# Output product by halves, with seven products in place of eight

## The chip, the cores and the metric

The kernel runs on one core of one Trainium2 chip. The metric is the device time of one execution in microseconds. The engines named below are TensorE (PE, with PEld for its weight loads), VectorE (DVE), ScalarE (ACT), GpSimd (POOL) and SyncE (SP), which issues nearly all transfers.

## The reference

One layer of a decoder on a sequence of 4096 tokens of width 1024. A normalised and modulated input h is projected; three groups of heads mix it (sliding-window attention, RWKV-7 and gated linear attention), each is multiplied by its own SiLU gate, and the groups side by side go through one output projection:

```python
    y = jnp.concatenate([attn, rwkv, gla], axis=-1) @ w_out
    return x + gate[:, None] * _rmsnorm(y, g_post)
```

The change is about this product, [4096 x 1024] by [1024 x 1024].

## The kernel before

All work is tiled by 256 tokens, 16 tiles (NS). A first pass over the tiles computes h and the two recurrent mixers and writes h (hscr) and the mixers' output (mscr) to device memory; besides, its stage_c (line 856) prepares weights for the second pass, one block a tile: a block of 1024 x 256 is read in eight pieces, its squares are summed, it is scaled by a power of two and split into a high and a low f16 part, and both are written to wscr. Blocks 7 to 10 of these eleven are w_out.

The second pass computes, tile by tile, the projections for attention and gates from hT (qkv, line 1531; gates, line 1577), the attention (stage_s, line 1592), the gated mixture (stage_m, line 1666) and the output product with its norm (outp, line 1701). stage_p2 (line 1733) gives TensorE's order in one tile: outp of the tile before, gates of this tile, qkv of the next; the attention of stage_s and the small sum of stage_m are put between.

Every large matmul is three f16 matmuls into one PSUM tile: high by high, high by low, low by high. In outp the stationary operand is a 128 x 128 block of the gated mixture (mT, tokens by depth), the moving one 256 columns of w_out: for each of two token halves and four column blocks, eight slices of depth with three matmuls each (proj_tok, line 512). Two column blocks share a PSUM tile of 512 columns; there are two such tiles, tag pj, which gates and qkv use as well. ScalarE or VectorE scales each block by its own factor oi into yv; a square with a sum, a reciprocal root by steps (rsqrt, line 415), a multiplication by gn and the addition of x follow, and the row block is stored.

stage_m, ahead of it, loads mscr into the upper half of mx, multiplies by the gates (ag), sums the squares of the whole tile, forms a power of two from the sum (pow2, line 425) and splits mx into mT, two halves of depth at a time. All four blocks of w_out, high and low, stay in SBUF: eight loads at line 1760. gn, the product of the post norm's weight and the adaLN gate, is formed in stage_v (line 1504) from three loads issued by ScalarE.

The order on each engine is written out by hand: emit (line 533) runs the stages' generators against a model of the clock, every operation is noted with a rank (its place in the program plus a lag), and Order.pin goes through all operations with estimated durations, takes on each engine the one of lowest rank that is ready, and fixes that order by dependencies. It covers TensorE, VectorE, ScalarE, POOL and SP; a transfer that is issued by ScalarE directly (nc.scalar.dma_start) is not noted. Each engine, SP too, then works its list in order and waits where an operand is not there. A flag decides after the first pass whether a slow path for one mixer runs (tc.If); in these runs it doesn't.

## Time and profile before

| what | us |
|---|---|
| median of 3 runs | 2195.03 |
| lowest and highest run | 2191.54, 2196.71 |
| the profiled execution's own time | 2192.24 |
| its span, first to last instruction | 2190.5 |

The page gives busy times of one profiled execution of this program; its time is 1.7 us longer than its span and 2.8 us below the median. Times in views are microseconds from the span's start, durations of one instruction in nanoseconds. A matmul's duration holds its way through the array, so throughput is read from the distance of starts. Nearly all instructions bear line 319, the helper that records them: groups are told apart by the names of their tiles.

### The profile page before, as it was taken

The page shows a single profiled execution, that of the slowest core. Times are in us where ns is not written, and L with a number is a line of the kernel's source. Part 1 is how long each engine was busy: PE and PEld are TensorE (multiplying, and loading weights), DVE is VectorE, ACT ScalarE, POOL GpSimd, SP SyncE. Part 2 cuts the span into 40 slices and gives each one's busy share as a digit, 9 for nine tenths or more (in the row PEclk, how much of TensorE's full clock was granted, in tenths as well). Part 3 has the DMA queues.
Part 4 walks back from the last instruction along what each step waited for, and adds up shares of the span by engine and source line. Part 5 has one row for each costly group of instructions (what it writes and reads, how often), then busy time and mean ns, then how long its engine had stood idle before and what let it go on. Part 6 is the DMA issues. An engine that isn't in the chain of part 4 may idle for free. (4 is left out here: it accounts for less than half of the span.)

```text
span 2190.5 us, 61819 instructions
## 1 busy us (share of the span) xinstructions
PE 2075.6 (95%) x25469; PEld 1770.8 (81%) x25469; DVE 1486.5 (68%) x4959; ACT 1109.3 (51%) x2645; POOL 203.0 (9%) x404
## 2 busy tenths in 40 slices
PE   4999999999999999999887999999999999999996
PEld 4778877888887878877566888888888888888885
DVE  6677777777687776876645767656666666666764
ACT  3966676667675766665133434434343444433442
POOL 0011111111101111123500000000000000000000
PEclk9999999999999999999788999999999999999998
DMA  9232323132223231333333121111221211212111
GB/s 314 87 104 80 99 92 103 38 96 86 88 83 99 90 99 32 106 122 112 97 121 120 59 81 61 63 66 65 76 73 64 79 52 61 81 69 81 61 42 40
DMA packets 162420, 188.50 MB, mean 86 GB/s; under 512 B 49857, under 2 KB 133331, under 8 KB 157909
## 3 DMA queue, kind: packets, MB, share of 16 engines
q1 hardware_dynamic: 160100, 182.23, 25.3%
q8 instruction: 202, 3.31, 0.6%
q10 hardware_dynamic: 2032, 2.26, 0.3%
q14 instruction: 86, 0.70, 0.1%
HBM read 126.75 MB, written 57.68 MB: 84 GB/s over the span
## 5 line engine op out<-in xcount | busy, mean ns | idle before, releaser
L319 PEld LDWEIGHTS <-mT 128*128 128x128 f16 x3072 | 301.3, 98 | 39.1 <-ACT mT L319 2.6
L319 ACT ACTIVATE pr<-pr,nm,lsc 128x256 f32<-128x256 f32 (+1 forms) x256 | 149.3, 585 | 86.2 <-DVE nm L319 86.2
L319 ACT ACTIVATE ag<-gp,gh 128x512 f32<-128x512 f32 x64 | 43.6, 682 | 183.3 <-PE gp L319 183.3
L319 DVE CUSTOM_DVE_ANT_0 pr<-sc,ab,sinks 128x256 f32<-128x256 f32 (+1 forms) x256 | 107.7, 476 | 36.6 <-PE sc L319 34.6
L319 PEld LDWEIGHTS <-hT 128*128 128x128 f16 x1536 | 116.4, 98 | 18.6 <-DVE hT L319 1.7
L319 DVE SCALAR_TENSOR_TENSOR ag<-ag,gp 128x512 f32<-128x512 f32 x64 | 43.4, 678 | 111.6 <-ACT ag L319 111.5
L319 PE MATMUL pv<-gvh,hT 128*128 128x272 f16 x512 | 98.9, 282 | 0.9 <-DVE hT L319 0.8
L319 PE MATMUL qp<-hT,q1h 128*128 128x256 f16 x512 | 88.4, 278 | 8.3 <-DVE kT L319 8.3
L319 PE MATMUL op<-o0h,mT 128*128 128x256 f16 x512 | 93.3, 276 | 2.8 <-ACT mT L319 2.5
L319 POOL COPY kT<-kT 128x512 f16<-128x512 f16 x15 | 9.2, 612 | 923.8 <-DVE kT L319 859.4
L319 PE MATMUL zz<-hT,kh 128*128 128x256 f16 x512 | 93.1, 275 | 0.0
L319 ACT ACTIVATE jy<-yv 128x1024 f16<-128x1024 f32 x32 | 33.8, 1056 | 113.8 <-DVE yv L319 113.8
L319 PE MATMUL op<-o3h,mT 128*128 128x256 f16 x512 | 91.4, 273 | 0.0
L319 PE MATMUL gqk<-hT,gqkh 128*128 128x256 f16 x512 | 87.8, 273 | 3.4 <-DVE zb L319 2.7
L319 PE MATMUL op<-o2h,mT 128*128 128x256 f16 x512 | 89.3, 273 | 0.0
L319 PE MATMUL lp<-hT,Lh 128*128 128x256 f16 x512 | 89.0, 273 | 0.1
L319 PE MATMUL op<-o1h,mT 128*128 128x256 f16 x512 | 89.1, 273 | 0.0
L319 PE MATMUL zz<-hT,rh 128*128 128x256 f16 x512 | 89.1, 276 | 0.0
L319 PE MATMUL zz<-hT,vh 128*128 128x256 f16 x512 | 88.1, 273 | 0.0
L319 PE MATMUL gp<-hT,q3h 128*128 128x256 f16 x512 | 86.7, 275 | 0.0
L319 PE MATMUL qp<-hT,q0h 128*128 128x256 f16 x512 | 86.6, 275 | 0.0
L319 ACT ACT_TABLE_LOAD x65 | 83.4, 1283 | 5.3 <-DMA sinks<-in_rows 4.2
(416 smaller groups left out, 6365.4 us busy)
## 6 DMA issues: line engine op xcount, KB each, us to landing
xt<-in_x SPq DMA_DIRECT2D x16, 1024.0 KB, 5.7
hscr<-hT SPq DMA_DIRECT2D x16, 1024.0 KB, 5.1
hT<-hscr SPq DMA_DIRECT2D x16, 1024.0 KB, 4.8
xo<-in_x SPq DMA_DIRECT2D x16, 1024.0 KB, 5.6
out<-yv SPq DMA_DIRECT2D x32, 512.0 KB, 3.1
cs<-in_w SPq DMA_DIRECT2D x112, 128.0 KB, 2.2
cs<-in_wo SPq DMA_DIRECT2D x64, 128.0 KB, 2.3
v<-vscr SPq DMA_DIRECT2D x128, 64.0 KB, 1.9
```

The source lines that it names most:

```text
L319: r = f(*args, **kw)
```

## The change

Mixture and w_out are cut into halves, a11 to a22 (tokens by depth) and w11 to w22 (depth by columns), each product of a block pair is 128 tokens by 512 depth by 512 columns, and the eight block products become seven, of sums and differences (the Winograd form of Strassen's identity). Seven weight sets (w11, w21, w22, and four combinations) are formed in the first pass: wo_squares sums the squares of all of w_out in tiles 7 and 8, and wo_group forms, splits and writes a strip of 128 rows and 128 columns of each quarter, 16 groups in tiles 9 to 14, with four subtractions on POOL. One scale holds for all of w_out.

In the second pass stage_m keeps the mixture in two tiles (mxa, mxb), squares each half by itself, and forms four combinations of the token blocks on POOL, three of them in place. block splits one operand [128 x 4 x 128] into high and low; four such tiles go round, so the first four are split in stage_m and the other three in outp, each after the product that frees its tile. outp runs seven products of 12 matmuls with 512 columns, each into one pj tile; a copy by ScalarE and seven additions by VectorE form the four quarters of y. The copy and the additions are noted with a rank lower by 150 (URGENT). Four weight sets stay in SBUF; the other three go in turn through one buffer (Wv), each half of which is loaded anew, 512 KB, as soon as its matmuls are issued. The factor oi is one column now and enters in the norm. x comes in two loads of 128 rows into one buffer, and gn lies beside that buffer, formed in stage_v with two loads of rows through SP into it, one after the other. ag is one tile for all. Of block, stage_m, outp and norm only the new text is shown; what it replaces stands above.

```diff
+URGENT = 150
...
-            self.model.order.lag = LAG.get(self.model.stage, 0)
+            self.model.order.lag = LAG.get(self.model.stage, 0) - self.model.order.urgent
...
-    wscr = dp.tile([11, P, 2, KD * 256], F16, name="wscr")
+    wscr = dp.tile([7, P, 2, KD * 256], F16, name="wscr")
+    woscr = dp.tile([7, P, 2, KD // 2, 512], F16, name="woscr")
...
-    w_inv = [cp.tile([P, 1], F32, name=f"winv{n}") for n in range(11)]
+    w_inv = [cp.tile([P, 1], F32, name=f"winv{n}") for n in range(8)]
+    wo_ss = cp.tile([P, 4 * KD], F32, name="wo_ss")
+    wo_sc = cp.tile([P, 1], F32, name="wo_sc")
...
+        def wo_squares(h):
+            for j in range(16 * h, 16 * h + 16):
+                s32 = wt([P, 256], "cs", 2)
+                SP.dma_start(s32, wo[:, j * 256 : (j + 1) * 256])
+                yield [s32]
+                S.activation(wt([P, 256], "ch", 2, F16), s32, AF.Square, accum_out=wo_ss[:, j : j + 1])
+            if h == 0:
+                return
+            sst = st.tile([P, 1], F32, tag="wss", name="wss")
+            V.tensor_reduce(sst, wo_ss, axis=AX.X, op=ALU.add)
+            yield [sst, "mq"]
+            sp = mq("wssp")
+            PE.matmul(sp[:, 0:1], ones, sst, start=True, stop=True)
+            tot = st.tile([P, 1], F32, tag="wtot", name="wtot")
+            V.tensor_copy(tot, sp[:, 0:1])
+            pow2(wo_sc, w_inv[7], tot)
+        def wo_group(k, c):
+            left, right = [wt([P, 256], "cs", 2) for _ in range(2)]
+            for t, k8 in ((left, k), (right, 4 + k)):
+                for h in range(2):
+                    col = c * P + h * 512
+                    at = (col // 256) * 2048 + k8 * 256 + col % 256
+                    SP.dma_start(t[:, h * P : (h + 1) * P], wo[:, at : at + P])
+            w11, w12, w21, w22 = left[:, 0:P], left[:, P:], right[:, 0:P], right[:, P:]
+            yield [left, right]
+            def parts(t, p):
+                m = t.shape[-1] // P
+                hi, lo = wt([P, 256], "ch", 2, F16)[:, 0 : m * P], wt([P, 256], "cl", 2, F16)[:, 0 : m * P]
+                S.activation(hi, t, AF.Identity, scale=wo_sc)
+                V.scalar_tensor_tensor(lo, t, wo_sc, hi, op0=ALU.mult, op1=ALU.subtract)
+                for n, z in enumerate((hi, lo)):
+                    SP.dma_start(woscr[p : p + m, :, n, k, c * P : (c + 1) * P].rearrange("m p c -> p m c"),
+                                 z.rearrange("p (m c) -> p m c", m=m))
+            parts(w11, 0)
+            parts(right, 1)
+            G.tensor_tensor(w11, w12, w11, op=ALU.subtract)
+            G.tensor_tensor(w12, w22, w12, op=ALU.subtract)
+            yield [left]
+            parts(left, 3)
+            G.tensor_tensor(w22, w22, w11, op=ALU.subtract)
+            G.tensor_tensor(w21, w21, w22, op=ALU.subtract)
+            yield [right]
+            parts(right, 5)
...
-            for n in range(11):
-                if n % (NS - 1) != i:
+            if 7 <= i < 9:
+                yield from wo_squares(i - 7)
+            elif 9 <= i < NS - 1:
+                for g in range(i - 9, 16, 6):
+                    yield from wo_group(g % 4, g // 4)
+            for n in range(7):
+                if n != i:
                     continue
-                src = w2[:, n * 2048 : (n + 1) * 2048] if n < 7 else wo[:, (n - 7) * 2048 : (n - 6) * 2048]
+                src = w2[:, n * 2048 : (n + 1) * 2048]
...
     def stage_v(_):
-        bgx = t_x("bgn")
         nc.scalar.dma_start(gn, gscr[0:1, :].to_broadcast([P, D]))
         for a in range(2):
-            nc.scalar.dma_start(bgx[:, a, :], rows[1 + a : 2 + a, :].to_broadcast([P, D]))
-        V.tensor_add(gn, gn, bgx[:, 0, :])
-        V.tensor_mul(gn, gn, bgx[:, 1, :])
-        yield
+            SP.dma_start(xo, rows[1 + a : 2 + a, :].to_broadcast([P, D]))
+            yield [xo]
+            V.tensor_tensor(gn, gn, xo, op=(ALU.add, ALU.mult)[a])
...
-        ag = t_A([P, 8, NT], "ag")
+        ag = t_A([P, 8, NT], "ag") if i == 0 else F[0]["ag"]
...
+    def block(i, n):
+        f = F[i]
+        t = blocks[len(split) % len(blocks)]
+        split.append((i, n))
+        f["blk"].append(t)
+        S.activation(t[:, 0], f["src"][n], AF.Identity, scale=f["msc"])
+        V.scalar_tensor_tensor(t[:, 1], f["src"][n], f["msc"], t[:, 0], op0=ALU.mult, op1=ALU.subtract)
     def stage_m(i):
         yield [("s", i), ("gates", i), ("o", i - 1)]
         f = F[i]
+        ag, half = f["ag"], [f["mx"], wt([P, 4, NT], "mxb", 1)]
+        SP.dma_start(half[1].rearrange("p b n -> p (b n)"), mscr[i])
+        yield [*half, ag]
+        mss = st.tile([P, 2], F32, tag="mss", name="mss")
+        f["blk"] = []
+        for j in range(2):
+            for n in (2 * j, 2 * j + 1):
+                z = half[j][:, 2 * (n % 2) : 2 * (n % 2) + 2, :].rearrange("p b n -> p (b n)")
+                V.scalar_tensor_tensor(z, z, g_h[n], ag[:, 2 * n : 2 * n + 2, :].rearrange("p b n -> p (b n)"),
+                                       op0=ALU.mult, op1=ALU.mult)
+            S.activation(blocks[(len(split) + j) % len(blocks)].rearrange("p a k n -> p (a k n)"),
+                         half[j].rearrange("p k n -> p (k n)"), AF.Square, accum_out=mss[:, j : j + 1])
         done.add(("og", i))
         yield [mss, "mq"]
         mp = mq("mp")
+        PE.matmul(mp[:, 0:2], ones, mss, start=True, stop=True)
         mtot = st.tile([P, 1], F32, tag="mtot", name="mtot")
+        V.tensor_reduce(mtot, mp[:, 0:2], axis=AX.X, op=ALU.add)
+        msc = f["msc"] = st.tile([P, 1], F32, tag="msc", name="msc")
         miv = st.tile([P, 1], F32, tag="miv", name="miv")
         pow2(msc, miv, mtot)
+        oi = f["oi"] = st.tile([P, 1], F32, tag="oi", name="oi")
+        V.tensor_mul(oi, miv, w_inv[7])
+        (a11, a21), (a12, a22) = [[h[:, :, t * P : (t + 1) * P] for t in range(2)] for h in half]
+        s1 = wt([P, 4, P], "sm1", 1)
+        f["src"] = [a11, a12, a11, s1, a21, a22, a12]
+        G.tensor_tensor(s1, a21, a22, op=ALU.add)
+        G.tensor_tensor(a21, a11, a21, op=ALU.subtract)
         yield [msc]
+        block(i, 0)
+        G.tensor_tensor(a11, s1, a11, op=ALU.subtract)
+        block(i, 1)
+        G.tensor_tensor(a12, a12, a11, op=ALU.subtract)
+        yield [a11]
+        for n in range(2, len(blocks)):
+            block(i, n)
+    def load_o(t, n):
+        for h in range(2):
+            SP.dma_start(t[:, :, 2 * h : 2 * h + 2, :], woscr[n, :, :, 2 * h : 2 * h + 2, :])
+    PRODUCTS = ((0, False), (1, True), (6, True), (3, False), (4, True), (5, True), (2, False))
     def outp(i):
         f = F[i]
+        x2 = xo if i < NS - 1 else t_hT("xo2").rearrange("p a k n -> p (a k n)").bitcast(F32)
+        SP.dma_start(x2[:, 0:D], x[i * NT + P : (i + 1) * NT, :])
         yield [("m", i)]
+        yv = [wt([P, D], "yv", 2) for _ in range(2)]
+        c1, c2 = slice(0, 512), slice(512, 1024)
+        def product(po, n):
+            yield [f["blk"][n]]
+            A, (w, stays) = f["blk"][n], PRODUCTS[n]
+            W = Wr[w] if stays else Wv
+            for k in range(KD // 2):
+                for a, b in ((0, 0), (0, 1), (1, 0)):
+                    PE.matmul(po, A[:, a, k, :], W[:, b, k, :], start=k == a == b == 0,
+                              stop=k == KD // 2 - 1 and a == 1)
+                if k == 1 and not stays:
+                    later = [m for m, s in PRODUCTS[n + 1 :] + PRODUCTS[: n + 1] if not s][0]
+                    if n < 6 or i < NS - 1:
+                        SP.dma_start(Wv[:, :, 0:2, :], woscr[later, :, :, 0:2, :])
+                if k == 3 and not stays and (n < 6 or i < NS - 1):
+                    SP.dma_start(Wv[:, :, 2:4, :], woscr[later, :, :, 2:4, :])
+                yield
+            if n + len(blocks) < 7:
+                block(i, n + len(blocks))
+        def full(n):
+            yield ["pj"]
+            po = pjt("op")
+            yield from product(po, n)
+            f["po"] = po
+        def add(to, z):
+            model.order.urgent = URGENT
+            V.tensor_tensor(to, f["po"], z, op=ALU.add)
+            model.order.urgent = 0
+        (y11, y12), (y21, y22) = [[y[:, c1], y[:, c2]] for y in yv]
+        yield from full(0)
+        model.order.urgent = URGENT
+        S.copy(y21, f["po"])
+        model.order.urgent = 0
+        yield from full(1)
+        add(y11, y21)
+        yield from full(2)
+        add(y21, y21)
+        yield from full(3)
+        add(y12, y21)
+        yield from full(4)
+        add(y22, y12)
+        add(y21, y21)
+        yield from full(5)
+        add(y21, y21)
+        norm(i, 1, yv[1], x2[:, 0:D], f["blk"][5])
+        if i < NS - 1:
+            SP.dma_start(x2[:, 0:D], x[i * NT : i * NT + P, :])
+        else:
+            SP.dma_start(x2[:, D : 2 * D], x[i * NT : i * NT + P, :])
+        yield from full(6)
+        add(y12, y12)
+        norm(i, 0, yv[0], x2[:, 0:D] if i < NS - 1 else x2[:, D : 2 * D], f["blk"][6])
         done.add(("o", i))
+    def norm(i, a, yv, xt, junk):
+        oi = F[i]["oi"]
+        sy = st.tile([P, 1], F32, tag="sy", name="sy")
+        S.activation(junk.rearrange("p a k n -> p (a k n)"), yv, AF.Square, scale=oi, accum_out=sy)
+        V.tensor_scalar(sy, sy, 1.0 / D, 1e-6, op0=ALU.mult, op1=ALU.add)
+        ry = st.tile([P, 1], F32, tag="ry", name="ry")
+        rsqrt(ry, sy, 1)
+        V.tensor_mul(ry, ry, oi)
+        V.scalar_tensor_tensor(yv, yv, ry, gn, op0=ALU.mult, op1=ALU.mult)
+        V.tensor_add(yv, yv, xt)
+        SP.dma_start(out[i * NT + a * P : i * NT + (a + 1) * P, :], yv)
...
-    for n in range(4):
-        Wo.append(load_2(7 + n, wb.tile([P, KD, 256], F16, name=f"o{n}h"), wb.tile([P, KD, 256], F16, name=f"o{n}l")))
+    Wr = {}
+    for n, stays in PRODUCTS:
+        if stays:
+            Wr[n] = wb.tile([P, 2, KD // 2, 512], F16, name=f"o{n}")
+    Wv = wb.tile([P, 2, KD // 2, 512], F16, name="ov")
+    tiles_o = [(Wv, 0), *((Wr[n], n) for n, stays in PRODUCTS if stays)]
+    for t, n in tiles_o:
+        load_o(t, n)
...
+    x2 = t_x("x2")
+    xo, gn = x2[:, 0, :], x2[:, 1, :]
+    mtp = t_A([P, 4, 2, 4, P], "mtp", F16)
+    blocks, split = [mtp[:, n] for n in range(4)], []
```

80 lines of the change are left out of this document (14 added, 66 removed).

## The prediction

> **What bounds the kernel now.** I read the page's head and its forty slices, then a table by stage, then who waited for whom on TensorE.
>
> ```profile
> span 2190.5 us, 61819 instructions
> PE 2075.6 (95%) x25469; PEld 1770.8 (81%) x25469; DVE 1486.5 (68%) x4959; ACT 1109.3 (51%) x2645; POOL 203.0 (9%) x404
> PE   4999999999999999999887999999999999999996
> PEclk9999999999999999999788999999999999999998
> ```
>
> The reader sees TensorE full from the second slice on, with one dent in the middle, where the first pass hands over to the second, and a weak last slice. The output product lies wholly to the right of the dent. The table by stage (stretch, length, busy time of each engine, clock, DMA) says how full:
>
> ```profile
> 475.00:1000.00 525.00, 511.25 (x7002) 420.98 (x7001) 389.66 (x1395) 339.06 (x787) 84.57 (x171) 1.00 0.29 88
> 1217.00:2147.00 930.00, 924.32 (x10717) 825.78 (x10716) 602.17 (x1798) 382.41 (x971) 7.96 (x13) 1.00 0.20 68
> 1501.66:1566.39 64.73, 64.42 (x748) 57.57 (x747) 41.58 (x124) 26.59 (x68) 0.61 (x1) 1.00 0.20 69
> ```
>
> The second row is the second pass: TensorE idles 5.7 of 930 us at full clock. The third is one of its tiles, from one load of hT to the next: period 64.73 us, TensorE idle 0.31, VectorE busy 41.58. So TensorE's own work sets the time there, and a matmul column removed is time removed, unless a wait takes its place. Few waits stand beside it (TensorE from 1190 us on):
>
> ```profile
> PE sc L319 <- DVE m L319: 8.3, 1, 8.3
> PE qp L319 <- DVE kT L319: 5.7, 14, 1.7
> PE mp L319 <- ACT mT L319: 4.4, 1, 4.4
> PE op L319 <- ACT mT L319: 2.5, 1, 2.5
> ```
>
> The first is one stall in the dent, the last two are the lead-in of the last tile, and none is paid in every tile but the second, 0.4 us.
>
> **The product itself.** Per tile 192 matmuls of 256 columns go (2 token halves, 4 column blocks, 8 slices of depth, 3 part products; 3072 in 16 tiles), and 84 of 512 come (7 products, 4 slices, 3 part products).
>
> ```profile
> L319 PEld LDWEIGHTS <-mT 128*128 128x128 f16 x3072 | 301.3, 98 | 39.1 <-ACT mT L319 2.6
> 1263.16 16.37 PE op L319 x150
> 1515.27 0.28 PE L319 MATMUL vp<-q2h,hT 128*128 128x128 f16 x2
> 1517.61 0.28 PE L319 MATMUL vp<-q2h,hT 128*128 128x128 f16 x2
> ```
>
> The second row, from the chain that ended last, gives 16.37/150 = 0.1091 us for 256 columns. Between the last two starts lie 42 matmuls of 128 columns: 2.34/42 = 0.0557. So 128 columns more cost 0.0534, a matmul's fixed part is 0.0023, and 512 columns are estimated at 0.2159 us (no such f16 matmul is in the trace; the bounds are 4 x 0.0534 = 0.2136 and 2 x 0.1091 = 0.2182). Per tile 192 x 0.1091 = 20.95 becomes 84 x 0.2159 = 18.14: 2.81 us less, in 16 tiles **45.0 us less** (42.0 to 48.1). A weight load of 98 ns stays under a matmul of 216.
>
> **What VectorE and ScalarE take over.**
>
> ```profile
> L319 DVE SCALAR_TENSOR_TENSOR ag<-ag,gp 128x512 f32<-128x512 f32 x64 | 43.4, 678 | 111.6 <-ACT ag L319 111.5
> L319 DVE SCALAR_TENSOR_TENSOR mx<-mx,gh,ag 128x512 f32<-128x512 f32 x64 | 45.3, 749 | 1.8 <-ACT mx L319 0.8
> L319 DVE SCALAR_TENSOR_TENSOR mT<-mx,msc,mT 128x1024 f16<-128x1024 f32 x32 | 39.6, 1278 | 1.1 <-ACT mT L319 1.1
> L319 DVE TENSOR_SCALAR yv<-op,oi 128x256 f32<-128x256 f32 x64 | 28.0, 478 | 29.2 <-PE op L319 29.2
> L319 DVE STREAM_TRANSPOSE pr<-pr 128x1024 f32<-128x1024 f32 x62 | 76.8, 1238 | 0.6
> L319 DVE SCALAR_TENSOR_TENSOR yv<-yv,ry,gn 128x1024 f32<-128x1024 f32 x32 | 41.1, 1285 | 1.1
> L319 ACT ACTIVATE mT<-mx,msc 128x1024 f16<-128x1024 f32 x32 | 35.0, 1140 | 7.7 <-DVE msc L319 7.7
> L319 ACT ACTIVATE mT<-mx 128x2048 f16<-128x2048 f32 x16 | 30.6, 1910 | 41.2 <-DVE mx L319 39.7 <-issue 1.5
> L319 POOL TENSOR_TENSOR qb<-qg,bdm 128x512 f32<-128x512 f32 x32 | 35.4, 1126 | 50.7 <-DVE qg L319 50.5
> ```
>
> VectorE gets 7 adds from PSUM (0.68, as ag) and 7 block splits (0.75, as mx), 10.0 us, and loses two mT (2 x 1.28) and four yv (4 x 0.48), 4.5: 5.5 us more, 47.1 of a period of 61.9, or 76%. It stays below TensorE. ScalarE's splits go from 2 x 1.14 to 7 x 0.57, half of one each, its squares read the same columns, and its four evacuations become one copy: under 2 us more, with 38 free. Both cost nothing by their sum; what can cost is when they come.
>
> A **bank** now holds one product for 84/7 x 0.2159 = 2.59 us, where it held two column blocks for 48 x 0.1091 = 5.24. There are two banks, so a product must be added away within 2.59 us of its end, less 0.68 for the add and some 0.2 of signals: 1.7 us are left to wait for VectorE, 1.0 where one product is added twice. The longest instruction it can meet is 1.29. One in the way is covered, but not where two adds follow; the adds' rank is lifted by 150, so they pass all that is ready. Bounds: 0, and 0.3 us in each of 112 products (1.29 - 1.0, paid everywhere), 33 us. Nearest is the existing wait on q and k, 0.4 us a tile, where VectorE also clears the banks; I take half, 0.2 us a tile: **+3 us**.
>
> **The weights.** Three of seven sets come through one buffer, two halves of 512 KB each.
>
> ```profile
> mx<-mscr SPq DMA_DIRECT2D x16, 512.0 KB, 5.0
> out<-yv SPq DMA_DIRECT2D x32, 512.0 KB, 3.1
> 1518.54 0.38 SPq L319 DMA_DIRECT2D vscr<-vt  x1
> 1520.38 4.71 SPq L319 DMA_DIRECT2D v<-vscr  x8
> 1518.71 0.27 PE L319 MATMUL op<-o0h,mT 128*128 128x256 f16 x1
> ```
>
> A half is asked for when its old content is used (after slice 1, after slice 3) and needed two products plus half a product later: 1.30 + 5.18 = 6.5 us, more where score matmuls run between. A landing takes 3.1 to 5.0. So it is covered, if SP issues at once. SP waits in order: behind a half stand the stores of out and the eight v loads, and those occupy SP from 1520.4 to 1525.1 just as the product runs. The first half can be issued at about 1518.7 + 1.3 = 1520.0, ahead of them; the second, ready 2.2 us later at the earliest, comes behind, at 1525.1, and lands by 1528.2 to 1530.1; product four's second half starts at 1518.7 + 7.8 + 1.3 = 1527.8, plus two groups of score matmuls (16 x 0.109 = 1.7), 1529.5. Bounds 0 and 0.6 us a tile, 10 us; I take 0.1: **+2**. The third streamed set has nothing of that kind ahead of it, the first has the other 40 us of the period.
>
> **Stage m.** Blocks need four POOL operations (1.13 each), but the first and second product need at most one of them. Two half squares and a split of 512 columns replace one square of 2048 and splits of 1024, so the first block is ready earlier than mT was.
>
> ```profile
> 1513.13 2.47 DVE L319 SCALAR_TENSOR_TENSOR mT<-mx,msc,mT 128x1024 f16<-128x1024 f32 x2
> 1560.93 0.77 ACT L319 COPY mx<-ovp 128x128 f32<-128x128 f32 x4 [0.57 <-PE ovp L319]
> 1567.11 0.69 DVE L319 SCALAR_TENSOR_TENSOR ag<-ag,gp 128x512 f32<-128x512 f32 x1 [3.91 <-ACT ag L319]
> ```
>
> mT is done at 1515.60, 3.1 us before the product at 1518.71: that is the cover, **0**. It is gone if POOL and VectorE hinder each other (rival 5). The attention chain ends (mx, 1561.7) 6.1 us before the last gate (ag, 1567.8) and loses 2.8 of that, as the gates move up; VectorE's additions delay it by at most 5.5 us, which leaves 0.9 of m's cover: 0.
>
> **The dent.**
>
> ```profile
> 1182.62 0.86 ACTq L1509 DMA_DIRECT2D bgn<-in_rows  x2
> 1190.14 1.23 DVE L319 TENSOR_TENSOR gn<-gn,bgn 128x1024 f32<-128x1024 f32 x1 [10.90 <-DMA bgn<-in_rows]
> 1193.71 1.01 PE L319 MATMUL sc<-kT,q 128*128 128x256 f16 x4 [8.29 <-DVE m L319]
> 1190.00:1200.00 10.00, 6.29 (x38) 4.77 (x38) 8.84 (x25) 2.85 (x5) 0.00 (x0) 0.58 0.59 200
> ```
>
> VectorE stands with gn's first add at the head of its queue until 1190.14; behind it stand the maxima of the scores, and TensorE waits 8.29 us, then runs at clock 0.58. The planner does not see loads issued by ScalarE, so it put that add first. The change loads the two rows through SP, which it does see: the add moves behind the scores. A second load must then wait for the first add, and VectorE may stand for it, but TensorE has two banks of gates (10.5 us) to do. Bounds: 0 gained, and 8.3 + 2.6 (6.29 busy us at clock 0.58 are 3.65 at full) = 10.9 gained; I take **-6**, half of it and a little, since the cause is seen but the new order is not.
>
> **First pass.** The weights' preparation becomes 32 squares and 16 groups, spread over eight tiles. Three groups a tile are 12 splits on ScalarE and on VectorE, each under half a microsecond (estimated from mx, twice to four times as wide), 12 short additions on POOL and 36 short DMAs. The first row of the stages has TensorE busy 511.25 of 525, VectorE 389.66, ScalarE 339.06: TensorE idles 1.7 us per 65. Bounds: 0, and a quarter more idle in eight tiles, 3.4: **+1**.
>
> **The end.**
>
> ```profile
> 2153.32 0.38 PE L319 MATMUL mp<-mss,ones 128*128 128x1 f32 x2 [4.37 <-ACT mT L319]
> 2157.51 22.35 PE op L319 x188
> 2185.68 1.22 DVE L319 TENSOR_TENSOR yv<-yv,xo 128x1024 f32<-128x1024 f32 x1
> ```
>
> The last tile has no cover. Its lead-in shortens by about 2 us (half a square 0.95, halves of both splits 0.57 + 0.64). After the last matmul at 2179.9 the norm ends at 2186.9; in the new order the other rows' norm (0.68 + 2.5) overlaps it: 2 us later. **0**, bounds -2 and +2.
>
> **Sum**, against the profiled execution, 2192.24 us (span 2190.5 and 1.7 around it): 2192.2 - 45.0 + 3 + 2 - 6 + 1 = 2147.2. That execution lies 2.8 under the median of the runs shown, so I forecast **2150 us**. With the better ends (no waits, all of the dent, 2 us at the end) it is 2134; with no gain in the dent, 0.3 us a tile of waits for banks and as much for weights, and the worse ends of the rest, 2163; with the median's offset 2137 to 2166.
>
> **Rivals.**
> 1. *The streamed set is late.* If both halves go behind the eight v loads, the first lands at 1525.1 + 5.0 = 1530.1 and is needed at 1528.2: 1.9 us in 15 tiles, +28 in place of the 2: 2176. For it: SP is in order, and the loads fall just there. Against: the first half is ready before v.
> 2. *Slower: banks cleared late.* If VectorE's written order puts two long instructions (2 x 1.26) or a wait of its own ahead of the adds, each product waits 2.5 + 0.7 + 0.2 - 2.6 = 0.8 us: 112 x 0.8 = 90 us in place of the 3: 2237. It decides from 45/112 = 0.4 us a product. For it: VectorE keeps its order and is busy 22.53 of 32 us around the product:
>
> ```profile
> 1518.50:1550.50 32.00, 32.00 (x362) 28.47 (x360) 22.53 (x82) 14.21 (x47) 0.00 (x0) 1.00 0.17 55
> ```
>
> Against: the lifted rank. The clock could fall too: the trace has that after an idle time of 8.29 us, while a tile with 0.31 us of idle time keeps 1.00. The Trainium skill, TensorE: Matmul & The Clock Gate, section "A second HAM failure mode: psum-queue depth-cycling", tells of a kernel with 512 columns in which short idle times at bank changes brought the slow clock back again and again; no run here shows that yet.
> 3. *No change.* If the attention chain with 5.5 us more of VectorE, not TensorE, sets the period, it stays near 64.7: 2190 to 2199. Against: 6.1 us of slack, 23 us of VectorE idle in a tile.
> 4. *It doesn't do what it says*: 512 columns at 0.2182 would give 3 us back, 2153, inside the forecast.
> 5. *POOL and VectorE shut each other out* in stage m: the four additions, 4 x 1.13 = 4.5 us, come on top, 1.4 more than the cover of 3.1, in 16 tiles 22: 2172. For it: block splits read two operands from the same memory at the same time. Against: the trace has no second-pass stretch with both, and products one and two need one addition at most. The Trainium skill, SBUF — State Buffer, section "SBUF: two separate sides", says that a VectorE instruction with two SBUF inputs and a GpSimd one that reads SBUF exclude each other for a whole instruction; no run here shows it so far.
>
> **Chances.** Forecast with 4: 0.72; rival 5: 0.05; rival 1: 0.08; rival 3: 0.05; rival 2: 0.10. The range, 2136 to 2174, takes in rival 5 and the milder part of rival 1 (0.03), and holds 0.80. A measurement of this kernel tells about 0.2%, 4.4 us, from no change. Faster 0.85, same 0.05, slower 0.10.
>
> **What would show it.** Op matmuls 0.216 us apart, 1344 of them; period near 62; TensorE's waits on op from VectorE under 0.3 us a tile, none long on the streamed buffer; VectorE 47 us a tile; no wait of 8 us at the dent. Waits of op above 0.4 us a product, or a clock below 1.00 in the second pass, would make it wrong.

## The result and the profile after

| what | before | after |
|---|---|---|
| median, us | 2194.67 (9 runs) | 2210.21 (9 runs) |
| lowest and highest run | 2179.43, 2199.69 | 2202.88, 2215.34 |
| the profiled execution's own time | 2192.24 | 2211.18 |

The ratio is 1.0086, 95% interval 1.0061 to 1.0112: the changed kernel is 0.9% slower. The forecast was 2150 us, and the range 2136 to 2174 does not hold the time.

The head and the slices of the page of the changed kernel, then its table by stage (stretch, length, busy time of TensorE, its weight loads, VectorE, ScalarE and POOL, clock, DMA share, GB/s) for one tile of the second pass, from one load of hT to the next, and the waits of TensorE from 1300 to 2020 us (sum, times, longest):

```profile
span 2209.3 us, 59345 instructions
PE 2059.9 (93%) x23735; PEld 1611.7 (73%) x23735; DVE 1593.0 (72%) x5076; ACT 1144.9 (52%) x2741; POOL 326.1 (15%) x532
PE   4999999999999999998978899999999999999996
PEclk8999999999999999999789999999999999999998
```

```profile
1586.88:1651.64 64.76, 62.68 (x640) 47.03 (x639) 47.36 (x131) 27.98 (x71) 6.38 (x5) 1.00 0.36 117
```

```profile
PE op L320 <- ACT vt L320: 15.3, 11, 1.4
PE sc L320 <- DVE m L320: 7.8, 12, 0.7
```

The period is 64.76 us, where it was 64.73: **in a tile of the second pass nothing was gained.** TensorE's busy time fell from 64.42 to 62.68, but its idle time rose from 0.31 to 2.08, and that is the two waits, 1.40 before the first product and 0.69 in the scores. The product itself is as short as expected: on the chain that ended last, 30 matmuls of 512 columns take 6.47 us, 0.2157 each.

```profile
2060.69 6.47 PE op L320 x30
```

Where the rest came from is read from loads that both kernels issue. First the last store of a mixer's result, then the fifth and the last load of hT, before and after:

```profile
1140.63 0.36 SPq L319 DMA_DIRECT2D mscr<-ysb  x1
...
1307.50 0.33 SPq L319 DMA_DIRECT2D hT<-hscr  x1
...
2019.51 0.33 SPq L319 DMA_DIRECT2D hT<-hscr  x1
```

```profile
1165.50 0.36 SPq L320 DMA_DIRECT2D mscr<-ysb  x1
...
1327.83 0.33 SPq L320 DMA_DIRECT2D hT<-hscr  x1
...
2040.21 0.33 SPq L320 DMA_DIRECT2D hT<-hscr  x1
```

The last mixer ends 24.9 us later; at the fifth hT load 20.3 of that are left, at the last load 20.7, and the end, from there to the span's end, is 1.9 us shorter (169.1 for 171.0). So the whole 18.8 us are lost in the first pass, a few come back in the dent, and eleven tiles of the second pass give nothing.

### The profile page after: what moved, and what is told of

It reads as the page before. It is cut to its first block, busy times and chain, and to the rows that moved or that the text cites. A ratio compares the mean times of both kernels' runs of the same rounds, so it can differ in the third digit from the quotient of the medians.

```text
span 2209.3 us, 59345 instructions
## 1 busy us (share of the span) xinstructions
PE 2059.9 (93%) x23735; PEld 1611.7 (73%) x23735; DVE 1593.0 (72%) x5076; ACT 1144.9 (52%) x2741; POOL 326.1 (15%) x532
## 5 line engine op out<-in xcount | busy, mean ns | idle before, releaser
L320 PEld LDWEIGHTS <-mtp 128*128 128x128 f16 x1344 | 129.5, 98 | 165.3 <-ACT vt L320 21.4
L320 PE MATMUL op<-o,mtp 128*128 128x512 f16 x768 | 174.4, 380 | 0.0
L320 PE MATMUL op<-ov,mtp 128*128 128x512 f16 x576 | 142.8, 381 | 20.2 <-ACT vt L320 18.1
L320 POOL TENSOR_TENSOR sm<-mxa,mxb 128x512 f32<-128x512 f32 x16 | 20.3, 1270 | 758.9 <-DVE mxb L320 704.1
L320 DVE TENSOR_TENSOR yv<-op,yv 128x512 f32<-128x512 f32 x112 | 75.1, 681 | 59.8 <-PE op L320 57.5
L320 ACT ACTIVATE mtp<-yv,oi 128x1024 f16<-128x1024 f32 x32 | 36.5, 1141 | 135.7 <-DVE yv L320 134.2
L320 ACT ACTIVATE mtp<-mxa,msc 128x512 f16<-128x512 f32 x48 | 34.6, 721 | 103.0 <-PE op L320 59.2
L320 PE MATMUL gp<-hT,q4h 128*128 128x256 f16 x512 | 87.6, 276 | 0.0
```

What stands on the lines that cost most here:

```text
L320: r = f(*args, **kw)
```

## Experiments: the second pass

Dots in a diff mark lines that are left out. **Theory W**: the period is TensorE's work plus the waits at its banks, and each wait removed shortens it. **Rival C**: some other chain sets 64.7 us (rival 3 of the prediction), and a wait that goes turns up elsewhere. That the period stayed within 0.03 us speaks for C; the runs had to decide. The lines of one tile around the first product, on VectorE, POOL, ScalarE and TensorE of the changed kernel (start, duration, operation, out<-in, and in brackets the idle time before and what ended it):

```profile
1600.11 0.75 DVE L320 SCALAR_TENSOR_TENSOR mtp<-mxb,msc,mtp 128x512 f16<-128x512 f32 x1
1600.77 1.76 DVE L320 SCALAR_TENSOR_TENSOR mtp<-sm,msc,mtp 128x512 f16<-128x512 f32 x1
1602.57 0.69 DVE L320 SCALAR_TENSOR_TENSOR q<-qp,q 64x512 f16<-64x512 f32 x1
1603.28 0.93 DVE L320 SCALAR_TENSOR_TENSOR mtp<-mxa,msc,mtp 128x512 f16<-128x512 f32 x1
1604.24 0.69 DVE L320 SCALAR_TENSOR_TENSOR q<-qp,q 64x512 f16<-64x512 f32 x1
```

```profile
1600.34 1.65 POOL L320 TENSOR_TENSOR mxa<-sm,mxa 128x512 f32<-128x512 f32 x1 [5.45 <-DVE mtp L320]
1602.07 1.59 POOL L320 TENSOR_TENSOR mxb<-mxb,mxa 128x512 f32<-128x512 f32 x1
```

```profile
1603.90 0.47 ACT L320 ACTIVATE vt<-vp,winv 128x256 f32<-128x256 f32 x1
```

```profile
1605.03 1.24 PE L320 MATMUL op<-ov,mtp 128*128 128x512 f16 x5 [1.40 <-ACT vt L320]
```

The bracket names vt, but ScalarE was done with vt at 1604.37. The bank that the first product takes is the one that q used, and VectorE reads the last of q out of it until 1604.93, 0.1 us before the product starts. It comes late because it stands behind the block splits in VectorE's order, and of these the one that runs beside a POOL sum takes 1.76 us in place of 0.75, the other 0.93.

**q's splits lifted.** The splits of q get the additions' lift of 150.

```diff
+                model.order.urgent = URGENT
                 S.activation(d[hi], qp[hi], AF.Identity, scale=2.0**-13)
                 V.scalar_tensor_tensor(d[lo], qp[hi], 2.0**-13, d[hi], op0=ALU.mult, op1=ALU.subtract)
+                model.order.urgent = 0
```

> The two splits of q at the end of each tile's projections get the lifted rank (150) that the additions have; nothing else changes. Theory A (in each tile the first product waits 1.4 us because its PSUM tile is held by the last q, whose split stands in VectorE's queue behind three block splits): the wait of 1.40 us before the first product goes, the period of a tile falls from 64.76 to about 63.4, the time by about 20 us. Rival (the wait is for vt on ScalarE, as the row says, or for the blocks): the wait stays above 1 us and the period within 0.3 of 64.76.

2211.17 us, period 64.78. VectorE does q's splits and the block splits in the same order as before in every tile: by the planner's durations, which know nothing of POOL, a block split is always ready before q, and a rank only decides between operations that are ready. The run tells nothing for or against W.

**Sums before the scale is known.** S2 and S4 go to parts of yv that are free then, so that all four POOL sums run before the first split; with tiles of their own they do not fit into SBUF, where the last pool then needs 40 KB a partition and 36.6 are left. (The first pass has two other edits in this run: below.)

```diff
-        f["src"] = [a11, a12, a11, s1, a21, a22, a12]
+        f["yv"] = [wt([P, D], "yv", 2) for _ in range(2)]
+        s2, s4 = [y[:, 512:1024].rearrange("p (k n) -> p k n", k=4) for y in f["yv"]]
+        f["src"] = [a11, a12, s2, s1, a21, a22, s4]
         G.tensor_tensor(s1, a21, a22, op=ALU.add)
         G.tensor_tensor(a21, a11, a21, op=ALU.subtract)
+        G.tensor_tensor(s2, s1, a11, op=ALU.subtract)
+        G.tensor_tensor(s4, a12, s2, op=ALU.subtract)
         yield [msc]
...
```

> Two stages, read apart. Second pass: POOL forms all four sums of stage m before the scale is known (two of them in parts of the output tile that are free then), so that none runs beside a block split on VectorE. Theory W (the waits at the handover of banks are the lost time, and they add up): the splits of 1.76 and 0.93 us become 0.75, the wait of 1.40 us before the first product goes, and the period, 64.76 us, falls to 63.2 to 63.6. Rival C (another chain than TensorE's sets the period): the wait goes and turns up elsewhere, the period stays within 0.2 of 64.76. First pass: half the number of transfers and the groups spread over tiles 7 to 14, both at once. The 16th store of a mixer's result came at 1140.6 us before the change, at 1165.5 after it, at 1156.1 with fewer transfers alone and 1161.1 with the spread alone: 1152 if their gains add, 1156 if they are one gain.

Period 63.97, 0.79 less:

```profile
1584.18:1648.15 63.97, 62.38 (x640) 47.07 (x639) 46.91 (x131) 27.79 (x71) 5.59 (x5) 1.00 0.37 118
```

The groups of the third split, which reads s1, in the changed kernel, then of this split and of a sum on POOL in this run (name, times | busy us, mean ns | idle before):

```profile
L320 DVE SCALAR_TENSOR_TENSOR mtp<-sm,msc,mtp 128x512 f16<-128x512 f32 x16 | 27.6, 1725 | 0.0
```

```profile
L320 DVE SCALAR_TENSOR_TENSOR mtp<-sm,msc,mtp 128x512 f16<-128x512 f32 x16 | 11.9, 744 | 0.0
...
L320 POOL TENSOR_TENSOR yv<-sm,mxa 128x512 f32<-128x512 f32 x16 | 20.3, 1267 | 0.0
```

The split takes 0.74 again, and POOL's sums take 1.27 to 1.30, where the last two took 1.65 and 1.58. The wait before the first product is 0.71, since all four splits still stand ahead of q; the one in the scores is 0.88. TensorE idles 1.59 in place of 2.08, and its busy time is 0.30 less too. The period fell, against C, though by about half of what was expected (63.2 to 63.6).

**Sums on VectorE**, in both passes, by writing V for G in the eight lines.

> All sums of halves go from POOL to VectorE, in both passes. Second pass: four more additions of 512 columns (some 0.68 us each, 2.7 us a tile) on VectorE, and nothing of POOL beside the splits. Theory W with the exclusion as cause: splits at 0.75 us, the wait before the first product falls from 1.40 to below 0.7, period 63.4 to 64.2. Rival C: 64.76. Rival S (the wait is the queue on VectorE as such, not the exclusion): period 64.8 to 67.5, as the queue gets longer. First pass: 64 subtractions of 256 columns leave POOL's queue. If POOL's queue is what the mixers wait for there, the 16th store moves from 1165.5 us to 1145 to 1155; if it is the transfers or the place, it stays at 1162 or later.

Period 64.36, 0.40 less, although VectorE is 1.5 us busier in a tile (48.87). Without POOL the splits take 0.75, so it is POOL beside them and not VectorE's load that stretched them. The wait before the first product fell to 1.00 only, not below 0.7, and the period stays just above the 64.2 that W allowed: what left the queue as exclusion came back in part as sums ahead of q.

**No lift of the additions**, URGENT = 0.

> Second pass: the lift of the additions from PSUM is set to 0, so that they stand in program order with the score maxima. If the lift causes the 0.69 us wait of the scores, it goes, and the additions come later: theory W gives 64.1 if they are still in time (2.59 us a product), up to 68 if each product waits some 0.5 us for its bank. First pass: only one of the 16 groups of weights is made, and its parts are stored to all 16 places by 14 transfers, so the output product uses wrong weights; the 16 groups' work on ScalarE, VectorE, POOL and most of the transfers are left out, the 32 squares stay. If the groups cost the 25 us of the first pass, its 16th store returns from 1165.5 to 1140 to 1146 us; if squares or anything else do, it stays above 1155.

Period 67.32, of which TensorE idles 4.44; the waits of the scores stay. So the lift is worth 2.6 us a tile in this run (period 64.76 with it), and the prediction was right to lean on it.

**The first norm later.** The other wait, in the scores, begins on VectorE. In the changed kernel:

```profile
1625.43 0.15 DVE L320 TENSOR_SCALAR sy<-sy 128x1 f32<-128x1 f32 x1 [0.97 <-ACT mtp L320]
...
1625.89 0.48 DVE L320 CUSTOM_DVE_ANT_0 pr<-sc,ab,sinks 128x256 f32<-128x256 f32 x1
```

```profile
1626.83 0.60 PE L320 MATMUL sc<-kT,q 128*128 128x256 f16 x4 [0.69 <-DVE m L320]
```

VectorE stands 0.97 us at the first step of the norm of rows 128 to 255, which waits for ScalarE's square, with score maxima behind it, and TensorE waits for these. First try: the small steps after the last product in the program.

```diff
...
+        sy = square(i, yv[1], f["blk"][5])
         yield from full(6)
         add(y12, y12)
+        norm(i, 1, yv[1], x2[:, 0:D], f["blk"][5], sy)
...
```

> Second pass: the small VectorE steps of the first norm (the ones that wait for ScalarE's square, 0.97 us at the head of VectorE's queue with score maxima behind them) are put after the last product. Theory W: the 0.69 us wait of the scores goes, the period falls from 64.76 to 64.0 to 64.2. Rival C: 64.76. First pass: six transfers a group in place of twelve, and the subtractions on VectorE. With fewer transfers alone the 16th store came at 1156.1 us; if POOL's queue costs the rest it comes at 1141 to 1148, if not at 1153 to 1158.

Period 64.77. This looks like C, but the trace shows the same step at the same place, so the wait was never taken away:

```profile
1610.30 0.15 DVE L320 TENSOR_SCALAR sy<-sy 128x1 f32<-128x1 f32 x1 [0.97 <-ACT mtp L320]
```

**Both norms in one chain** of small steps on two columns. It needs the square of the last product's rows, and that is a dependency, not a rank.

```diff
...
+            sy = st.tile([P, 2], F32, tag="sy", name="sy")
+            square(i, yv[1], f["blk"][5], sy[:, 1:2])
             yield from full(6)
             add(y12, y12)
+            square(i, yv[0], f["blk"][6], sy[:, 0:1])
+            ry = inverse(i, sy, 2)
...
```

> Second pass alone is changed: the two norms of a tile share one chain of small steps on two columns, which needs both squares and so cannot stand ahead of the score maxima any more (putting only the first norm later in the program had left VectorE's order as it was). Theory W: the 0.97 us for which VectorE stood at the square's result goes, the 0.69 us wait of the scores goes with it, the period falls from 64.76 to 63.9 to 64.2. Rival C (another chain sets the period): 64.76 again, as after the first attempt. The first pass is as in the changed kernel, and the fifth tile's hT load should come within some 8 us of 1327.8.

The same table by stage, for one tile of this run, and TensorE's waits from 1300 to 2020 us: one of the two is gone.

```profile
1589.18:1653.09 63.91, 62.52 (x640) 46.99 (x639) 46.01 (x119) 27.96 (x71) 6.38 (x5) 1.00 0.36 118
```

```profile
PE op L320 <- ACT vt L320: 15.3, 11, 1.4
```

Period 63.91, 0.85 less, as W gives; TensorE idles 1.39, the wait that is left. C falls: two waits of different origin were shortened, one at a time, and both times the period went with them, by 0.85 for a wait of 0.69 and by 0.79 for 0.50 of waits in all; the rest, 0.16 and 0.30, left TensorE's busy time. That gain and loss had cancelled to 0.03 us was chance.

## Experiments: the first pass

The groups of weights run from 831 to 1021 us. From there on the pass falls behind: the last three stores of h come 3.7, 7.5 and 16.1 us later than before the change, the last store of a mixer 24.9. The mixer's transfers adr<-AT, eight in a row, and the load that follows them, in the second half of the pass, before and after:

```profile
928.28 3.65 SPq L319 DMA_DIRECT2D adr<-AT  x8
933.11 1.11 SPq L319 DMA_DIRECT2D AS<-adr  x2
```

```profile
937.40 0.46 SPq L320 DMA_DIRECT2D woscr<-ch  x1
937.96 0.42 SPq L320 DMA_DIRECT2D adr<-AT  x1
938.47 0.38 SPq L320 DMA_DIRECT2D woscr<-cl  x1
...
942.05 1.84 SPq L320 DMA_DIRECT2D adr<-AT  x4
...
946.83 2.04 SPq L320 DMA_DIRECT2D adr<-AT  x1
...
950.93 1.11 SPq L320 DMA_DIRECT2D AS<-adr  x2
```

From the first of the eight to the load behind them passed 4.8 us, now 13.0: SP sends the groups' loads and stores in between, and at a store it stands until the split is done, with the mixers' transfers behind it in its list. What SP waited for between 840 and 1060 us, before and after:

```profile
SPq L319 <- DVE AT L319: 44.5, 4, 27.2
...
SPq L319 <- ACT ch L319: 10.0, 11, 2.7
...
SPq L319 <- DVE cl L319: 5.7, 4, 3.2
```

```profile
SPq L320 <- ACT ch L320: 25.4, 20, 3.2
SPq L320 <- DVE cl L320: 15.2, 11, 5.1
```

Before, SP stood mostly waiting for the mixers (AT) and 15.7 us for splits (ch, cl); after, 40.6 us for splits and 0.2 for AT. The kernel before had short transfers for w_out too, 64 loads and 64 stores in this pass; the changed one has 96 and 128, and they come later. **Theory T**: the groups' short transfers cost the time. **Theory E**: their splits and subtractions do. A third, on the place: three groups a tile are too close together. The first pass scatters by several us: left unchanged, in two of the runs above, it has the fifth load at 1327.60 and 1333.53, where the changed kernel has 1327.83. So what counts below is the ratio of several runs, and single loads only where they differ by more.

**Half the transfers**: both columns of a quarter pair in one load, high and low of an operand in one store, six transfers a group.

```diff
-    woscr = dp.tile([7, P, 2, KD // 2, 512], F16, name="woscr")
+    woscr = dp.tile([P, 7, 2, KD // 2, 512], F16, name="woscr")
...
-                for n, z in enumerate((hi, lo)):
-                    SP.dma_start(woscr[p : p + m, :, n, k, c * P : (c + 1) * P].rearrange("m p c -> p m c"),
-                                 z.rearrange("p (m c) -> p m c", m=m))
+                SP.dma_start(woscr[:, p : p + m, :, k, c * P : (c + 1) * P].rearrange("p m n c -> p (m n) c"), z.rearrange("p m n c -> p (m n) c"))
...
```

> Only the transfers of the weight preparation change: a group of w_out issues 6 transfers in place of 12 (both column halves in one load, high and low parts of one or two sets in one store). Theory B1 (the first pass loses its 24 us because SP's list is full and the mixers' small transfers stand behind the group's): the sixteenth store of a mixer's ysb, at 1140.6 us before and 1165.5 after the change, comes back to below 1150. Rival B2 (it is the work of ScalarE, VectorE and POOL, or the bunching of the groups late in the pass): it stays above 1157.

2203.48 us in one run, period unchanged; the sixteenth store at 1156.13, between the two forecasts. The same kernel, ten runs:

> The changed kernel with six transfers a group in place of twelve, the same work otherwise; one look gave 2203.5 us, fifth hT load 1320.5. If the number of transfers on SP is the price, about 7 us of 17 come back: ratio 1.003 to 1.006 where the changed kernel has 1.0086. If the look was chance, 1.007 or more.

Ratio 1.0025, interval 1.0008 to 1.0043: about 0.6%, 13 us, come back, where 7 had been forecast. The edit changes more than a number: the order of woscr in memory, the loads' and stores' sizes, and one store now waits for both parts. SP did not stand less at the splits but more:

```profile
SPq L320 <- DVE ch L320: 60.2, 25, 6.2
```

So time that SP spends waiting is no measure of the price either. In one run with the weights' subtractions moved to VectorE as well (the first try with the norm later) the store came at 1149.37 and the fifth load at 1312.68, between the forecasts again. That move alone does little that shows: in the run with all sums on VectorE the store came at 1160.66 and the fifth load at 1326.62.

**Groups spread**: squares beside the first seven sets, two groups a tile in tiles 7 to 14.

```diff
...
-            if 7 <= i < 9:
-                yield from wo_squares(i - 7)
-            elif 9 <= i < NS - 1:
-                for g in range(i - 9, 16, 6):
+            if i < 7:
+                yield from wo_squares(i)
+            elif i < NS - 1:
+                for g in range(2 * (i - 7), 2 * (i - 7) + 2):
```

> Only the place of the weight preparation changes: the squares of w_out go beside the first seven blocks, the 16 groups two a tile into tiles 7 to 14, in place of 3 a tile from tile 9 on. Theory B2 (bunching): the sixteenth store of ysb, 1165.5 us after the change and 1140.6 before it, comes to below 1152. Theory B1 (SP's list, whose transfers are only fewer per tile here) expects a part of that, 1150 to 1160; if the sum of the added work counts, wherever it stands, it stays above 1160. The second pass keeps its period of 64.76.

2206.64 in one run, 4.6 us less, which is inside the scatter, and the store at 1161.08, above 1160, as if the place did not matter. Together with half the transfers (the first pass of the run with early sums) the store came at 1145.65, earlier than either forecast, and yet the fifth hT load at 1328.03, no earlier than in the changed kernel: there TensorE had 82 us of work between that store and the fourth hT load, where it has 63 in the changed kernel. So the store alone misleads. The place is decided further below.

**One group in place of 16** (first in the run without the lift, where the sixteenth store came at 1145.19, as forecast, and the fifth load at 1309.33; then by itself):

```diff
-                for g in range(i - 9, 16, 6):
-                    yield from wo_group(g % 4, g // 4)
+                if i == 9:
+                    yield from wo_group(0, 0)
```

The stores of its parts are those of the diff with to_broadcast further below.

> The changed kernel with one of the 16 groups of weights made, and its parts stored to all 16 places by 14 transfers (so the output product uses wrong weights); squares, second pass and all else stay. If the 16 groups cost what the first pass lost (fifth tile's hT load at 1327.8 against 1307.5 before), it comes at 1306 to 1312 here, and the time is 2190 to 2197 us, 0.998 to 1.002 of the kernel before. If the squares, the new layout of the memory or chance in the first pass cost it, the load stays above 1320 and the ratio above 1.005.

Ratio 1.0008, 0.9987 to 1.0029, and the mixer's eight transfers go undivided again:

```profile
935.19 3.65 SPq L320 DMA_DIRECT2D adr<-AT  x8
...
940.00 1.11 SPq L320 DMA_DIRECT2D AS<-adr  x2
...
1308.49 0.33 SPq L320 DMA_DIRECT2D hT<-hscr  x1
```

So the 15 groups left out cost 19 us of the 20 in the profile, 0.8% in timed runs; squares and layout cost nothing that shows. Which part of a group does was asked in three experiments:

```diff
             yield [left, right]
+            if k + c > 0:
+                for p, m in ((0, 1), (1, 2), (3, 2), (5, 2)):
+                    for n in range(2):
+                        SP.dma_start(woscr[p : p + m, :, n, k, c * P : (c + 1) * P], woscr[p : p + m, :, n, 0, 0:P])
+                return
```

> The changed kernel, but 15 of the 16 groups only move data: their four loads stay, and their eight stores copy the first group's parts from DRAM; splits and subtractions of these groups are left out, and the output product uses wrong weights. With one group alone (and 14 transfers for its stores) the fifth tile's hT load came at 1308.5 us and the kernel took 1.0008 of the one before; with all of it 1327.8 and 1.0086. Theory T (SP's short transfers cost the 17 us): load at 1322 or later, ratio 1.005 to 1.009. Theory E (the splits and subtractions on ScalarE, VectorE and POOL cost it): load at 1307 to 1313, ratio 0.999 to 1.003. Both in part: between.

Ratio 1.0111, 1.0059 to 1.0163 (four runs); load at 1329.54. Transfers without the engines' work can cost all of it. But these are not the same transfers: the copies read device memory where the stores read SBUF, and each takes SP 0.61 us where a store takes 0.38 (medians), some 27 us more for the 120, so this run sets an upper end for T, not its price.

```diff
-                    SP.dma_start(woscr[p : p + m, :, n, k, c * P : (c + 1) * P].rearrange("m p c -> p m c"),
-                                 z.rearrange("p (m c) -> p m c", m=m))
+                    for q in range(m if k == c == 0 else 0):
+                        SP.dma_start(woscr[p + q, :, n].rearrange("p k (c j) -> p (k c) j", j=P),
+                                     z[:, q * P : (q + 1) * P].unsqueeze(1).to_broadcast([P, 16, P]))
```

> The other half: all 16 groups are loaded, split and subtracted, but only the first one's parts are stored, to all 16 places by 14 transfers; 120 of the 128 short stores are left out, and the output product uses wrong weights. Theory T: load at 1306 to 1314, ratio 0.999 to 1.003. Theory E: load at 1320 or later, ratio 1.005 to 1.009. If neither half alone costs much, it is the two together in the same tiles.

Ratio 1.0067, 1.0043 to 1.0090; the profiled execution, the fastest of ten, has the load at 1318.03. That is theory E's number by the ratio, and between the two by the load; but the 64 loads are still in SP's list, and they stand there for splits too, since a load waits until its buffer has been split:

```profile
SPq L320 <- DVE cl L320: 37.7, 15, 6.3
```

The next run takes them out (its stores are those of the diff above):

```diff
+        lr = []
...
-            left, right = [wt([P, 256], "cs", 2) for _ in range(2)]
-            for t, k8 in ((left, k), (right, 4 + k)):
+            if not lr:
+                lr.extend(wt([P, 256], "cs", 2) for _ in range(2))
+            left, right = lr
+            for t, k8 in ((left, k), (right, 4 + k)) if k == c == 0 else ():
```

> The last quarter of the question: all 16 groups' splits and subtractions stay, but they work on the first group's loaded tiles again and again, and only the first group's parts are stored; 60 of the 64 loads and 120 of the 128 stores are left out, and the output product uses wrong weights. With the stores alone left out the fifth hT load came at 1318.0 and the ratio was 1.0067; with transfers alone 1329.5 and 1.0111; with one group 1308.5 and 1.0008. If SP's queue is the whole cause, the load comes at 1306 to 1311 and the ratio is 0.999 to 1.003; if the engines' work costs half by itself, 1315 to 1320 and 1.004 to 1.007. The subtractions now form one chain through the same tiles, so a late group can hold up the next, but no mixer.

Ratio 1.0032, 1.0011 to 1.0053: at the upper edge of what T gives; its profiled execution was the slowest of ten, with the load at 1326.49. Against one group the difference is 0.24%, and the intervals overlap. The runs side by side, with the transfers for w_out in SP's list in the first pass:

| kernel | transfers | splits and subtractions | ratio |
|---|---|---|---|
| before | 128 | of the kernel before | 1 |
| changed | 224 | all | 1.0086 |
| half the transfers | 128 | all | 1.0025 |
| copies for stores | 224 | one group | 1.0111 |
| stores of one group | 110 | all | 1.0067 |
| loads and stores of one group | 50 | all | 1.0032 |
| one group | 50 | one group | 1.0008 |

The engines' work without the transfers costs 0.0 to 0.5%; what comes on top, up to the 0.8%, needs transfers in SP's list, which speaks for T. But their number is not the price: 110 of them leave 0.67%, 128 leave 0.25%. Whether a transfer costs by standing for a split, by its own time on SP or by the place that the planner gives it stays open.

## Experiments: the dent, and a version with the repairs

**gn through SP in the kernel before**, with a point (yield) at which the planner may put other work first, nothing else:

```diff
-            nc.scalar.dma_start(bgx[:, a, :], rows[1 + a : 2 + a, :].to_broadcast([P, D]))
+            SP.dma_start(bgx[:, a, :], rows[1 + a : 2 + a, :].to_broadcast([P, D]))
+        yield [bgx]
...
```

> The kernel before, with nothing but the two rows of gn loaded through SP, and a point at which the planner may put other work ahead of the two steps on them. If the wait of 8.29 us in the dent is what the prediction took it for, it goes, and the kernel gains 4 to 10 us: 0.995 to 0.998 of the kernel before. If other chains of the dent end as late, it stays within 2 us.

The fifth hT load comes at 1300.68, 6.8 us earlier than before the change, and no wait of 8 us is left; ratio 0.9981, 0.9956 to 1.0005. But the last store of a mixer, ahead of the dent, comes 2.5 us earlier there too (1138.16 for 1140.63), so the dent itself gives 4.4. The size is at the low end of the forecast; that it is a gain at all the timed runs leave just open.

**All repairs**: early sums, norms together, half the transfers, the weights' subtractions on VectorE, and the third and fourth split made dependent on q by a copy of the scale that reads q:

```diff
...
         block(i, 1)
+        if i + 1 < NS:
+            yield [("qkv", i + 1)]
+            msq = st.tile([P, 1], F32, tag="mtot", name="msq")
+            V.scalar_tensor_tensor(msq, F[i + 1]["q"][:, 1, 3, NT - 1 :], 0.0, msc, op0=ALU.mult, op1=ALU.add)
+            f["msc"] = msq
...
```

> All repairs at once: sums before the scale, norms together, third and fourth block split only after the next tile's q is out of its bank, six transfers a group, subtractions of the weights on VectorE. Theory W, by addition: period 64.76 - 0.80 (measured with early sums) - 0.71 (the wait before the first product that remained) - 0.88 (the wait of the scores that remained) = 62.4, that is 31 us less in 13 tiles; the fifth tile's hT load, 1327.8 in the changed kernel, at 1312 to 1320 as with the same weights work before: together 2160 to 2175 us, 0.98 to 0.99 of the kernel before. Rival C: the period does not go below 63.9, and the time is 2180 to 2195.

2181.18 us, ratio **0.994**, 0.992 to 0.996: 0.6% faster than the kernel before. The mean period is (2011.15 - 1314.44)/11 = 63.34:

```profile
PE sc L320 <- DVE m L320: 9.7, 11, 0.9
```

```profile
1600.73 0.71 DVE L320 SCALAR_TENSOR_TENSOR mtp<-yv,msq,mtp 128x512 f16<-128x512 f32 x1
1601.54 1.29 DVE L320 TENSOR_TENSOR yv<-op,yv 128x512 f32<-128x512 f32 x2
1602.75 0.47 DVE L320 CUSTOM_DVE_ANT_0 pr<-sc,ab,sinks 128x256 f32<-128x256 f32 x1
```

The wait before the first product is gone, but that of the scores is back at 0.88, now behind a late split and two additions: 62.4 by mere addition of gains was too low. The time lies in the range that rival C gave (2180 to 2195) and outside W's, the period below the 63.9 that C allowed: the waits do set the period, but one that goes can in part turn up elsewhere.

**The same with the groups spread:**

> The kernel with all repairs (0.994 of the one before, fifth hT load at 1314.4 us), with the squares beside the first seven sets of weights and the groups in tiles 7 to 14, two a tile. If the crowding of three groups in a tile still costs something there, the load comes at 1305 to 1311 and the ratio is 0.990 to 0.992; if the place does not matter or the late tiles are the worse ones, 0.994 to 0.998.

Ratio 0.9999, 0.9974 to 1.0024, outside both ranges, the load at 1331.60. The spread costs 0.6% where it seemed to gain in one run. The sixteenth store comes at 1152.19, as with the groups packed (1152.27): the 17 us of the load are lost behind it, with 82 us of TensorE's work between that store and the fourth hT load in place of 63. The spread puts groups into tile 14, next to the pass's end; that this is the reason is not shown.

## Why the prediction was wrong

Between the sum of 2147.2 and the profiled 2211.2 lie 64 us. By the terms of the sum, at the fifth hT load about -10 had been forecast (two tiles' product, the dent, +1) and +20.3 came: 30. In eleven tiles 11 x 2.5 = 28 less had been forecast, and 0.4 more came: 28. The rest, 6, is in the last three tiles.

- **First pass, "+1".** The first failed step, 0.8% or 17 us by the run with one group. The bound was taken from TensorE's idle share and from the engines' busy time. "36 short DMAs" a tile were counted and then priced at nothing; no queue was named that they are moved into. SP's list is worked in order, and the mixers' chain goes through it: its eight transfers took 13.0 us to the load behind them in place of 4.8. That the groups cost the time is shown, and that more than the engines' work is in it; what each transfer costs is not.
- **Stage m, "0".** The second. The cover of 3.1 us was real for the first product's operand, but the delay went another way: the splits hold up q's, and q holds the product's bank. This is rival 5's mechanism, with 0.79 us a tile where it was removed alone, in place of 1.4, and through a bank and not through the operand. It had 0.05. The Trainium skill, SBUF — State Buffer, section "SBUF: two separate sides", says that a VectorE instruction with two SBUF inputs and a GpSimd one that reads SBUF shut each other out; the trace agrees: 1.76 for 0.75 us beside POOL's 1.65.
- **Banks, "+3".** The third. Between products the additions were in time, as reckoned; without the lift it would have been 41 us (2.56 x 16). What was not reckoned is the bank ahead of the first product, and a norm in the middle of the product whose first step waits at the head of VectorE's queue, 0.85 us a tile. "What is queued behind" was asked for the additions only.
- **Product, "-45".** The matmul was right (0.2157 for 0.2159), the term was not: TensorE's busy time in a tile fell by 1.74 for 2.81, and the 1.07 that are missing are 17 us in 16 tiles, as much as the first pass. Most of it is the attention's value product, busy for 3.7 us a tile in place of 2.9: the planner now cuts it into 8 and 72 matmuls in both halves of a tile; a piece of 8 takes 0.38 us from start to start in place of 8/80 of 1.43:

```profile
1538.34 1.43 PE L319 MATMUL ovp<-pr,v 32*64 32x128 f32 x80
```

```profile
1621.33 0.45 PE L320 MATMUL ovp<-pr,v 32*64 32x128 f32 x8
1621.71 1.25 PE L320 MATMUL op<-o,mtp 128*128 128x512 f16 x5
```

- **VectorE and ScalarE.** VectorE 47.36 us a tile for 47.1; ScalarE 27.98, 1.4 more, as said. **Weights, "+2"**: no wait on the streamed buffer shows. **Dent, "-6"**: from the last mixer's store to the fifth load 166.9 before, 162.3 after, and 162.5 with gn alone: 4.5 and 4.4 less. **End, "0"**: from the last gate matmul to the span's end 41.5 before and 39.6 after, where the product's own terms promised 2.5 less; some 0.5 are missing, so the 0 was about right. The worse ends as the prediction lists them add up to 2165 (2192.2 - 42.0 + 4.8 + 4.8 + 3.4 + 2.0), not 2163, which changes nothing.
- **Rivals.** Rival 3 named the period to 0.1 us, for the wrong reason: no attention chain sets it. Rival 2 did not come, nor the slow clock between tiles: with a wait of 1.4 us in each tile the granted clock stayed 1.00, so what is cited there has no instance in these rows. In the last tile, after waits of 3.47 and 2.07 us, it was 0.86 (0.89 before the change).

## What to carry to other kernels

Work taken off the engine that bounds a stage comes back as time only if whoever hands over its first bank, and whoever stands ahead of that one in its queue, keeps up: follow each bank one user back before pricing a shorter product. Price a transfer that is moved into a stage by the queue it joins and by the chain that goes through that queue, not by bytes or by idle engines alone, and leave the work out in one run to see what it costs. A rank in a planner cannot move an operation past another that its model takes to be ready earlier; a dependency can, and whether an edit changed the order is to be read before its time is.

## What the hardware showed that was not expected

The exclusion of VectorE and POOL depends on where VectorE reads. In the rows above the split from SBUF at 1600.77 ends 0.54 us after POOL's first sum does, having taken 1.76, and the one at 1603.28 ends 0.55 us after POOL's second; but q's split at 1602.57, which reads PSUM, takes its usual 0.69 us right beside POOL's second sum (1602.07 to 1603.66). In the other tiles of the second pass it takes 0.69 at that place too. POOL pays as well: 1.65 and 1.58 us (means) for a sum that takes 1.27 alone. Both sums end 1.13 us after the end of the split that ran when they began (1600.86 and 1602.53), and that split reads another tile than the sum, which speaks against a shared tile as the reason.
